# Dilated attention on even tokens, then odd ones, two heads at a time in the array's halves

## The chip, the core and the metric

The kernel runs on one core of a Trainium2 chip. The metric is the device time of one execution in microseconds (us); the profile's times are those of one profiled execution. Engines: TensorE (PE; PEld is its weight load), VectorE (DVE), ScalarE (ACT), GpSimd (POOL), SyncE (SP, which issues most DMAs).

## What is computed

A network on 256 tokens of 1024 channels: gated feed-forwards, a forgetting attention, a dilated attention and two mixing layers, all in float32. The change concerns the dilated attention (16 heads of 64 channels, three groups):

```python
DIL_CONFIGS = ((128, 1), (512, 4), (2048, 16))      # window, dilation

def dilated_group(q, k, v, window, dilation):
    # query t attends t, t-d, t-2d, ..., t-window
    ...
    logits = jnp.einsum("bqhd,bqkhd->bhqk", qb, kb) * scale
    logits = jnp.where(valid, logits, -jnp.inf)
    lse = jax.nn.logsumexp(logits, axis=-1)
    ob = jnp.einsum("bhqk,bqkhd->bqhd", jnp.exp(logits - lse), vb)
    return ob, lse

for g, (window, dilation) in enumerate(DIL_CONFIGS):
    q = apply_rope(rms_norm(proj[:, :, g, 0], q_gain[g]), cos, sin)
    k = apply_rope(rms_norm(proj[:, :, g, 1], k_gain[g]), cos, sin)
    o, lse = dilated_group(q, k, proj[:, :, g, 2], window, dilation)
alpha = softmax(lses over the groups)
o = sum(alpha * outs)          # then o @ w_out
```

The merge over the groups equals one softmax over the keys of all three groups, and so it is computed. With dilations 4 and 16 a query at an even token only sees keys at even tokens, one at an odd token only odd ones.

## The kernel before

Channels lie on partitions, tokens along the free axis. Every weight is split into two float32r parts (`whi` by ScalarE, `wlo` by VectorE, one pair for each unit of 128 x 1024), and each projection is three TensorE products: `hh,whi`, `hl,whi`, `hh,wlo` (for values `whi,hh` and so on; `oh` and `ol` hold the attention's outputs for the last projection). These are called plain products here. Everything else runs beside them: generators (`dil_qk`, `dil_norm`, `dil_head`) yield until the class `Clock` estimates that an instruction's operands are there, and so the order on every engine is fixed when the program is built. All instructions pass through one helper, so the profile gives one line for them all (L415), and the groups are told apart by tiles: `qk` are logits, `cst,ar` transposes, `ar` on 128*64 the outputs, `cst,rs` the spreading of the inverse sums.

In `dil` the queries and keys of two heads (a pair) come from three projection tiles; `head_in` and `head_norm` norm them, `dil_norm` turns them (rotary embedding, VectorE). `dil_head` then handles one head: six float32 products give the logits of queries 0 to 127 with keys 0 to 127 and of queries 128 to 255 with all 256 keys, in each of three groups, in three neighbouring banks of PSUM; VectorE adds the mask `dm` and takes the row minimum (two masked sums of 384 and 768 columns); ScalarE takes the exponential with its sum; TensorE transposes nine tiles of 128 x 128, ScalarE copies them back, TensorE multiplies them with the values (`pv`) and spreads the inverse sums (`inverse`). Head e of a pair has its channels on partitions 64 e to 64 e + 63, so its logits use the upper or lower half of the array's rows, and its outputs one half of the array's columns. `P` is held twice, so that the two heads of a pair overlap. `o_store` copies output and inverse (`ot`), multiplies them and splits the product into `oh` and `ol`. `attn_out` runs the last projection in four steps of two pairs, waiting until these are stored; `residual` adds it to `x` and prepares the next norm.

Of the kernel before, what the change touches and what calls it, by code (L numbers as in the profile page):

```python
# [26 lines left out]
I32 = mybir.dt.int32  # L27
# [39 lines left out]
def _weights(seg):  # L67
    """Chunks of one part of the network, each of one or two units: (key, number of units)."""
# [58 lines left out]

# which layer's modulation is worked out beside which of the first blocks
# [102 lines left out]
# columns of the tile that holds one value per channel  # L231
# [9 lines left out]
# columns of the tile of constants  # L241
# [8 lines left out]
# columns of the small matrices of a mixing layer  # L250
# [40 lines left out]
def _host_cst():  # L291
# [10 lines left out]
    d0, d1 = [], []  # L302
    for window, dil in ((128, 1), (512, 4), (2048, 16)):
        d0.append(np.where(ok0 & (q - cols[:, :128] <= window) & ((q - cols[:, :128]) % dil == 0), 0, NEG))
        t = q + 128
        d1.append(np.where(ok1 & (t - cols <= window) & ((t - cols) % dil == 0), 0, NEG))
    dm = np.ascontiguousarray(np.concatenate(d0 + d1, axis=1), np.float32)
# [74 lines left out]
GAP = 400               # the least wait of VectorE that is filled  # L382
QUIET = 9               # from which chunk of the last rows no weights are prepared
QUIET_POST = 1
RESIDUAL_AT = 2         # chunk of rows at which the residual's operands are prepared
ORDER = (0, 2, 1, 3, 4, 6, 5, 7)
# after which chunks of the products ahead of a norm's scale come sums of squares, all of them, the scale, and weights
LEAD = ({2: (None,)}, 2, 3, (2, 3))
LEAD_POST = ({6: (None,)}, 6, 7, (6, 7))
NRAW = 4                # chunks of weights that are loaded ahead  # L390
NU = 7                  # units of weights that are prepared ahead
UNIT = 1024


class Engine:
    """An engine's instructions, with an estimate of when they are done."""
# [24 lines left out]
class Clock:  # L421
    """Passes instructions on to the core's engines, and estimates (in ns) when their operands are there and
    when they are done, from shapes alone: the order of what runs beside the projections follows it."""

    GRAIN = 512
    LATE = {"pe": 60, "dve": 250, "act": 360, "pool": 200, "dma": 100}     # until other engines see a result
# [30 lines left out]
    def grains(self, ap):  # L457
        """The parts of a tile that an operand touches."""
# [7 lines left out]
    def ready(self, name, ins=(), outs=()):  # L466
        """When engine name can read ins and write outs."""
# [25 lines left out]
    def fill_gap(self, name, ins, outs):  # L493
        """Emits what can fill VectorE's time until an instruction's operands are there."""
# [19 lines left out]
    def tile(self, pool):  # L514
        """pool.tile, which records when the slot of a new tile gets free."""
# [24 lines left out]
class Stream:  # L540
    """The weights, in the order in which they are used: each is loaded ahead, and split into the part
    that float32r holds and the rest, which float32r holds as well."""

    def __init__(self, k, dram):
# [38 lines left out]
    def step(self, limit):  # L583
        """Prepares the next unit, if there is room for it."""
# [58 lines left out]
    def need(self, l, blk):  # L643
        """Emits what computes the modulation's tile blk of layer l."""
# [8 lines left out]
class K:  # L653
    def __init__(self, tc, ctx, a, out):
# [6 lines left out]
        self.free = set(range(8))      # banks of PSUM  # L661
# [25 lines left out]
    # -- small helpers -----------------------------------------------------  # L687
# [26 lines left out]
    def mm(self):  # L714
        """A bank of PSUM, for the projections."""
# [3 lines left out]
    def mm4(self):  # L719
        """Four banks that leave four neighbouring ones."""  # L720
# [1548 lines left out]
```

## Time and profile before

| | |
|---|---|
| median of 3 runs | 1943.55 us (1941.72 to 1943.92) |
| span of the profiled execution (no other time is given for it) | 1946.9 us |
| TensorE busy | 1891.6 us, 97% |
| VectorE busy | 1488.4 us, 76% |
| ScalarE busy | 1013.4 us, 52% |

The dilated block lies between about 767 and 1124 us. Busy shares are means over stages with different limits, so the stretch itself has to be read. A record of TensorE has a modelled end and overlaps the next one; what a product costs in a row of them is read from start to start. The granted clock is a share of full speed: 1.00 is 2.4 GHz, 0.50 is 1.2 GHz.

### The profile page before, as it was taken

To read this page: it belongs to the slowest core of one execution; us is meant where nothing else is said; L and a number is where in the kernel's file an instruction comes from. 1 tells how busy PE (TensorE), PEld (TensorE's weight loads), DVE (VectorE), ACT (ScalarE), POOL (GpSimd) and SP (SyncE) were. 2 spreads that over 40 slices of the span, in tenths; PEclk is the share of its full clock that TensorE was granted. 3 is DMA by queue.
4 is the path that set the end of the run, shared out by engine and by line. 5 is a ranking of instruction groups with operands and counts; after the bars stand their busy time and mean duration, and the time that the engine had idled before them with its cause. 6 is when DMAs were issued, how large, how long until landed. Compare 5 with 4: busy or idle time off the path is not lost.

```text
span 1946.9 us, 36564 instructions
## 1 busy us (share of the span) xinstructions
PE 1891.6 (97%) x15150; PEld 1814.4 (93%) x15150; DVE 1488.4 (76%) x2706; ACT 1013.4 (52%) x1721; POOL 35.5 (2%) x40
## 2 busy tenths in 40 slices
PE   6999999999999999999999999999999998999997
PEld 6999987899999999999989899999889998989997
DVE  6987795598779876767777585569779778969876
ACT  3534644554355445554455464444666555466553
POOL 0100000000000000000000000000000000000000
PEclk9999989999999999999999999999989998999998
DMA  9798373289858973433324175535236543325550
GB/s 373 298 350 322 131 282 109 93 306 362 326 178 298 341 298 130 174 115 125 130 88 143 74 261 205 212 130 188 94 128 217 186 157 127 137 84 191 199 195 23
DMA packets 54167, 378.67 MB, mean 194 GB/s; under 512 B 6096, under 2 KB 7600, under 8 KB 9072
## 3 DMA queue, kind: packets, MB, share of 16 engines
q1 hardware_dynamic: 52992, 373.20, 52.2%
q0 software_dynamic: 864, 3.00, 0.5%
q8 instruction: 118, 1.93, 0.4%
q14 instruction: 49, 0.40, 0.1%
q10 hardware_dynamic: 144, 0.13, 0.0%
HBM read 375.21 MB, written 1.05 MB: 193 GB/s over the span
## 4 chain that ended last, share of the span: by engine, by line
PE 72%; issue 20%; DVE 4%; ACT 2%; POOL 1%; DMA 0%; POOLq 0%; SPq 0%; DVEq 0%; ACTq 0%
PE banks L415 72%; DVE ar L415 1%; DVE wlo L415 1%; POOL rz L415 1%; DVE x L415 1%; ACT whi L415 1%; ACT hh L415 0%; DVE sq L415 0%; DMA x<-x 0%; DVE hl L415 0%; DVE ht L415 0%; ACT sq L415 0%; ACT L415 0%; DVE wraw L415 0%; ACT ar L415 0%
## 5 line engine op out<-in xcount | busy, mean ns | idle before, releaser
L415 PE MATMUL banks<-hh,whi 128*128 128x256 f32 (+1 forms) x2792 | 799.2, 286 | 7.6 <-ACT hh L415 4.7
L415 DVE TENSOR_TENSOR wlo<-wraw,whi 128x1024 fp32r<-128x1024 f32 x557 | 670.2, 1220 | 171.2 <-ACT whi L415 170.6
L415 PE MATMUL banks<-hh,wlo 128*128 128x256 f32 (+1 forms) x2792 | 789.4, 283 | 2.0 <-DVE wlo L415 2.0
L415 PE MATMUL banks<-hl,whi 128*128 128x256 f32 (+1 forms) x2792 | 790.1, 283 | 0.2
L415 ACT CAST whi<-wraw 128x1024 fp32r<-128x1024 f32 x557 | 570.3, 1048 | 177.5 <-DMA wraw<-w 92.2
L415 PEld LDWEIGHTS banks<-hh,whi 128*128 128x128 f32 x2792 | 531.2, 190 | 13.5 <-ACT hh L415 5.5
L415 PEld LDWEIGHTS banks<-hh,wlo 128*128 128x128 f32 x2792 | 531.2, 190 | 2.8 <-DVE wlo L415 2.8
L415 PEld LDWEIGHTS banks<-hl,whi 128*128 128x128 f32 x2792 | 531.4, 190 | 1.1 <-DVE hl L415 1.1
L415 PE MATMUL banks<-oh,whi 128*128 128x256 f32 x1312 | 372.7, 284 | 7.3 <-DVE x L415 3.8
L415 PE MATMUL banks<-ol,whi 128*128 128x256 f32 x1312 | 366.8, 280 | 0.0
L415 PE MATMUL banks<-oh,wlo 128*128 128x256 f32 x1312 | 366.4, 279 | 0.0
L415 PEld LDWEIGHTS banks<-oh,whi 128*128 128x128 f32 x1312 | 247.2, 188 | 14.0 <-DVE x L415 6.3
L415 PEld LDWEIGHTS banks<-ol,whi 128*128 128x128 f32 x1312 | 247.5, 189 | 0.2 <-DVE ol L415 0.2
L415 PEld LDWEIGHTS banks<-oh,wlo 128*128 128x128 f32 x1312 | 247.2, 188 | 0.0
L415 DVE CUSTOM_DVE_ANT_0 wraw<-wraw,cb 128x1024 f32<-128x1024 f32 x128 | 152.0, 1217 | 0.5 <-DMA wraw<-w 0.5
L415 ACT ACTIVATE sg<-banks 128x256 f32<-128x256 f32 x82 | 31.5, 385 | 175.4 <-PE banks L415 175.3
L415 PE MATMUL banks<-whi,hh 128*128 128x256 f32 x352 | 106.0, 301 | 1.6 <-ACT hh L415 1.4
L415 PE MATMUL banks<-whi,hl 128*128 128x256 f32 x352 | 101.3, 288 | 0.1
L415 PE MATMUL banks<-wlo,hh 128*128 128x256 f32 x352 | 100.9, 287 | 0.0
L415 ACT COPY ar<-banks 128x384 f32<-128x384 f32 (+5 forms) x110 | 47.4, 477 | 99.3 <-PE banks L415 96.0
L415 PE MATMUL banks<-ar 128*64 128x256 f32 (+4 forms) x456 | 90.9, 335 | 0.0
L415 DVE SCALAR_TENSOR_TENSOR cy<-cs,vec,cy 128x255 f32<-128x255 f32 (+1 forms) x176 | 83.7, 481 | 7.8 <-ACT cy L415 4.7
(204 smaller groups left out, 1790.5 us busy)
## 6 DMA issues: line engine op xcount, KB each, us to landing
wraw<-w SPq DMA_DIRECT2D x342, 1024.0 KB, 4.9
ar<-w SPq DMA_DIRECT2D x8, 1024.0 KB, 10.4
wraw<-w SPq DMA_DIRECT2D x5, 512.0 KB, 3.4
ar<-lw POOLq DMA_DIRECT2D x2, 752.0 KB, 5.0
x<-x SPq DMA_DIRECT2D x1, 1024.0 KB, 7.2
out<-x SPq DMA_DIRECT2D x8, 128.0 KB, 1.9
cst<-cst SPq DMA_DIRECT2D x1, 595.5 KB, 6.1
ar<-dm POOLq DMA_DIRECT2D x1, 576.0 KB, 10.4
```

Source lines behind the costliest of these rows:

```text
L415: return f(out, *args, **kw)
```

## The change

The tokens are put in another order for the dilated block: even ones first, then odd ones. The norm ahead of it reads `x` in that order, the rotary tables are made in it, and the residual behind it writes `x` back in the old order. Now queries 0 to 127 are the even tokens and 128 to 255 the odd ones; group 0 (dilation 1) takes all 256 keys for each, groups 1 and 2 one tile of 128 keys. A generator handles a pair of heads at once, with each product of the first head next to the same one of the second. A masked sum now has 512 columns, and there are four for a pair; there are 16 transposes for a pair instead of 18. One pair is in flight at a time.

```diff
+def parted(ap):
+    return ap.rearrange("p (i b) -> p b i", b=2)
+def halves(ap):
+    return ap.rearrange("p (b i) -> p b i", b=2)
...
-    def make_h(self, rb, g, shift=None, ks=range(8)):
+    def make_h(self, rb, g, shift=None, ks=range(8), part=False):
+        order, same = (parted, halves) if part else (lambda t: t,) * 2
-            nc.vector.scalar_tensor_tensor(t, self.x[:, k], g[:, k:k + 1], rb[:, :S], op0=OP.mult, op1=OP.mult)
+            nc.vector.scalar_tensor_tensor(same(t), order(self.x[:, k]), g[:, k:k + 1], order(rb[:, :S]), op0=OP.mult,
+                                           op1=OP.mult)
...
-            nc.scalar.activation(self.hh[:, k], self.x[:, k], AF.Copy, scale=g[:, k:k + 1])
+            nc.scalar.activation(same(self.hh[:, k]), order(self.x[:, k]), AF.Copy, scale=g[:, k:k + 1])
...
+            x = order(self.x[:, m])
+            nc.vector.scalar_tensor_tensor(x, same(acc[bank][:, m % 2 * 256:m % 2 * 256 + 256]), gate[:, m:m + 1], x,
+                                           op0=OP.mult, op1=OP.add)
...
+    def inverse2(self, out, rs):
+        for qt in range(2):
+            for e in range(2):
+                self.nc.tensor.matmul(out[64 * e:64 * e + 64, qt * 128:qt * 128 + 128],
+                                      rs[:, 2 * e + qt:2 * e + qt + 1].to_broadcast([128, 64]), self.c("ident"),
+                                      start=True, stop=True, skip_group_check=True)
...
+    def dil_heads(self, c, qks, dv, vready, pvs):
+        while self.busy:
+            yield
...
+        for qt in range(2):
+            q = slice(qt * 128, qt * 128 + 128)
+            L = yield from self.bank(2)
+            for g, c0, keys in ((0, 0, slice(S, 2 * S)), (1, 256, slice(S + qt * 128, S + qt * 128 + 128)),
+                                (2, 384, slice(S + qt * 128, S + qt * 128 + 128))):
+                for e, r in enumerate(half):
+                    nc.tensor.matmul(L[:, e, c0:c0 + keys.stop - keys.start], qks[g][r, q], qks[g][r, keys], start=True,
+                                     stop=True)
+            for e in range(2):
+                p = P[:, e, qt * 512:qt * 512 + 512]
+                yield from self.on("dve", L[:, e], out=[p])
+                nc.vector.tensor_tensor_reduce(p, L[:, e], self.dm[:, qt * 512:qt * 512 + 512], -1.0, CAP, OP.add, OP.min,
+                                               nm[:, 2 * e + qt:2 * e + qt + 1])
...
+        for i, (g, kt) in enumerate(((0, 0), (0, 1), (1, 0), (1, 1), (2, 0), (2, 1))):
+            for e in range(2):
+                o = pv[64 * e:64 * e + 64, :S] if g == 0 else pv[64 * e:64 * e + 64, kt * 128:kt * 128 + 128]
...
+                nc.tensor.matmul(o, dv[:, g, kt, vh:vh + 64], p, start=i == 0, stop=g == 2, skip_group_check=True)
+        self.busy.remove(0)
+        self.inverse2(pv[:, S:], rs)
```

Where this stands in TensorE's order, at the logits of the second pair (`qk` with its number is the tile of a group, three of them; `hh`, `hl`, `whi`, `wlo` are a projection). Before:

```order
L415 MATMUL banks_70<-hh_74,wlo_9278 128x256
L415 MATMUL banks_70<-qk_8858 128x128
L415 MATMUL banks_70<-qk_8858 128x256
L415 MATMUL banks_70<-qk_8859 128x128
L415 MATMUL banks_70<-qk_8859 128x256
L415 MATMUL banks_70<-qk_8860 128x128
L415 MATMUL banks_70<-qk_8860 128x256
```

The second head's six follow in the same way. After:

```order
L425 MATMUL banks_70<-hh_74,wlo_9306 128x256
L425 MATMUL banks_70<-qk_8858 128x256 x2
L425 MATMUL banks_70<-qk_8859 128x128 x2
L425 MATMUL banks_70<-qk_8860 128x128 x2
L425 MATMUL banks_70<-qk_8858 128x256 x2
L425 MATMUL banks_70<-qk_8859 128x128 x2
L425 MATMUL banks_70<-qk_8860 128x128 x2
L425 MATMUL banks_70<-hh_74,whi_9305 128x256
```

Every x2 is the first head's product and the second's; the first three rows are the even queries, the next three the odd ones.

On ScalarE, at the end of the block, around the outputs of the last pair (`ar` from banks are the transposes copied back, `ot` output and inverse, `oh` what the last projection reads, `whi` a weight cast). Before:

```order
L415 CAST whi<-wraw 128x1024
L415 COPY ar<-banks 128x384
L415 COPY ot<-banks 128x512
L415 CAST whi<-wraw 128x1024
L415 CAST oh<-ot 128x256
```

After:

```order
L425 COPY ar<-banks 128x512 x4
L425 CAST whi<-wraw 128x1024
L425 CAST hh<-modc 128x8x2
L425 COPY ot<-banks 128x512
L425 CAST whi<-wraw 128x1024 x3
L425 CAST oh<-ot 128x256
```

Three weight casts instead of one now stand between `ot` and `oh`.

## Rows read from the trace of the kernel before

**Rows 1.** Busy time by stretch, attention part and after the idle time; first row: columns
```profile
core 0: us, PE busy (x) PEld busy (x) DVE busy (x) ACT busy (x) POOL busy (x), PEclk, DMA share, GB/s
780.00:1104.60 324.60, 324.60 (x2481) 297.75 (x2479) 231.18 (x439) 162.18 (x291) 0.00 (x0) 1.00 0.35 124
...
1107.70:1111.10 3.40, 3.31 (x14) 3.14 (x15) 1.64 (x4) 0.76 (x3) 0.00 (x0) 0.50 0.84 308
```
**Rows 2.** Waits of TensorE, 767 to 1104 us: total us, times, longest
```profile
PE banks L415 <- POOL rz L415: 0.4, 1, 0.4
```
**Rows 3.** Timeline of TensorE (start, us, instruction): logits of two heads, of one
```profile
898.70 3.65 PE L415 MATMUL banks<-qk 64*128 64x128 f32 x24
...
1082.44 0.28 PE L415 MATMUL banks<-oh,wlo 128*128 128x256 f32 x1
...
1082.80 0.28 PE L415 MATMUL banks<-oh,wlo 128*128 128x256 f32 x1
1083.01 2.23 PE L415 MATMUL banks<-qk 64*128 64x128 f32 x12
```
**Rows 4.** Timeline of TensorE: outputs, inverses, transposes of one head
```profile
908.85 2.17 PE L415 MATMUL banks<-ar 128*64 128x256 f32 x12
910.85 0.60 PE L415 MATMUL banks<-cst,rs 128*64 128x128 f32 x4
911.38 1.20 PE L415 MATMUL banks<-cst,ar 128*128 128x128 f32 x9
912.41 0.27 PE L415 MATMUL banks<-cst,ypad 128*96 128x128 f32 x1
```
**Rows 5.** Timeline of TensorE in a mixing layer, outputs on either 64 partitions
```profile
1332.90 1.14 PE L415 MATMUL banks<-ar,sv 128*64 128x128 f32 x16
1333.97 0.48 PE L415 MATMUL banks<-ar 128*128 128x256 f32 x1
```
**Rows 6.** Chain that ended last (start, us, what), and TensorE's timeline at its end
```profile
1104.12 0.59 ACT ot L415
1104.71 0.95 ACT whi L415
...
1105.68 1.22 DVE wlo L415
1106.91 0.35 DVE ot L415
...
1107.33 0.41 ACT oh L415
...
1107.79 0.58 PE L415 MATMUL banks<-oh,whi 128*128 128x256 f32 x1 [3.15 <-ACT oh L415]
```
**Rows 7.** Groups, 800 to 1104 us: count | busy us, mean ns | idle before
```profile
L415 DVE TENSOR_TENSOR wlo<-wraw,whi 128x1024 fp32r<-128x1024 f32 x65 | 78.4, 1220 | 28.8 <-ACT whi L415 28.7
L415 DVE TENSOR_TENSOR qk<-qk,ar 128x512 f32<-128x512 f32 x24 | 16.6, 692 | 0.8
L415 DVE CUSTOM_DVE_ANT_0 ar<-banks,ar 128x768 f32<-128x768 f32 x16 | 15.2, 953 | 0.0
L415 DVE CUSTOM_DVE_ANT_0 ar<-banks,ar 128x384 f32<-128x384 f32 x16 | 8.9, 556 | 15.8 <-PE banks L415 15.8
...
L415 ACT CAST whi<-wraw 128x1024 fp32r<-128x1024 f32 x64 | 65.8, 1058 | 0.2
L415 ACT ACTIVATE ar<-ar,nm 128x768 f32<-128x768 f32 x16 | 14.9, 934 | 1.1 <-DVE nm L415 1.0
```
**Rows 8.** Busy time by stretch in the forgetting attention, columns as in rows 1
```profile
240.00:280.00 40.00, 38.30 (x278) 35.04 (x277) 39.21 (x84) 24.35 (x42) 2.95 (x6) 0.94 0.79 288
274.80:285.00 10.20, 10.20 (x45) 9.29 (x44) 9.93 (x31) 3.92 (x10) 0.00 (x0) 0.50 0.64 237
```
**Rows 9.** Groups, 754 to 782 us, at the norm ahead of the dilated attention
```profile
L415 ACT ACTIVATE hh<-x,modc 128x256 fp32r<-128x256 f32 x6 | 3.0, 508 | 3.2 <-DVE x L415 3.2
...
L415 DVE SCALAR_TENSOR_TENSOR x<-banks,modc,x 128x256 f32<-128x256 f32 x5 | 2.4, 474 | 0.0
```

More of the change, by code (lines that the diff above doesn't have):

```diff
@@ L301, in _host_cst @@
     c["causal"] = np.concatenate([np.where(ok0, 0, NEG), np.where(ok1, 0, NEG)], axis=1)
[L302 to L307, printed above, removed]
+    dm = []
+    for qt in range(2):
+        for (window, dil), keys in zip(((128, 1), (512, 4), (2048, 16)), (range(2), (qt,), (qt,))):
+            for kt in keys:
+                lag = 2 * q + qt - (2 * np.arange(128)[None, :] + kt)
+                dm.append(np.where((lag >= 0) & (lag <= window) & (lag % dil == 0), 0, NEG))
+    dm = np.ascontiguousarray(np.concatenate(dm, axis=1), np.float32)
     row = np.arange(128) % 32
@@ L943, in mod, with ahead @@
         return self.modc[:, i + 1], self.modc[:, i]
-    def ahead(self, lead, g, shift):
+    def ahead(self, lead, g, shift, part=False):
         nc = self.nc
@@ L951, in ahead @@
         add, end, fold, merge = self.squares(st)
+        order, same = (parted, halves) if part else (lambda t: t,) * 2
         if shift is not None:
@@ L957, in high @@
         def high(k):
[L958 removed]
+            nc.scalar.activation(same(self.hh[:, k]), order(self.x[:, k]), AF.Copy, scale=g[:, k:k + 1])
         def low(k):
[L961 to L964 removed]
+            nc.vector.scalar_tensor_tensor(same(self.hl[:, k]), order(self.x[:, k]), g[:, k:k + 1],
+                                           same(self.hh[:, k].bitcast(F32)), op0=OP.mult, op1=OP.subtract)
+        return add, merge, fold, high, low, (st, end, g, shift, lead, part)
     def begin(self, norm, checks, lazy=False):
         nc = self.nc
[L970 removed]
+        st, end, g, shift, lead, part = norm
         n = S if shift is None else SX
@@ L993, in begin @@
                 self.st.step(NU)
-        nc.scalar.copy(self.rb, rb[:, :S])
+        if part:
+            nc.scalar.copy(halves(self.rb), parted(rb[:, :S]))
+        else:
+            nc.scalar.copy(self.rb, rb[:, :S])
         if not lazy:
-            self.make_h(rb, g, shift, ORDER)
+            self.make_h(rb, g, shift, ORDER, part)
         self.rel(rb)
@@ L1042, in rows, with residual @@
         self.quiet = False
-    def residual(self, gate, *following):
+    def residual(self, gate, following, part=False):
         nc = self.nc
+        order, same = (parted, halves) if part else (lambda t: t,) * 2
         self.qm = QUIET
-        add, merge, fold, high, low, norm = self.ahead(LEAD, *following)
+        add, merge, fold, high, low, norm = self.ahead(LEAD, *following())
         late = []
@@ L1206, in ffn @@
                            {1: self.rope_tables, 2: lambda: self.mix_ahead(0)}[l + j]() if l else None)
[L1207 removed]
+        norm, after = self.residual(self.gate(l, s, 0.5), following)
         end(after)
@@ L1216, in attn_out @@
             if c == RESIDUAL_AT:
-                norm, after = self.residual(gt, *following())
+                norm, after = self.residual(gt, following, part=l == 1)
             for half in range(2):
@@ L1525, in dil_qk @@
         ready[i] = "in"
-    def dil_head(self, h, qks, dv, vready, pvs):
+    def dil_heads(self, c, qks, dv, vready, pvs):
         nc = self.nc
-        e = h % 2
-        r = slice(64 * e, 64 * e + 64)
-        P, pT = self.PP[e], self.PT
-        while e in self.busy:
+        half = [slice(0, 64), slice(64, 128)]
+        P, X = self.P2, self.X2
+        while self.busy:
             yield
-        self.busy.add(e)
-        nm, sm, rs = self.small(2, "nm"), self.small(2, "sums"), self.small(2, "rs")
+        self.busy.add(0)
+        nm, sm, rs = self.small(4, "nm"), self.small(4, "sums"), self.small(4, "rs")
@@ L1537, in dil_head @@
         yield from self.on("pe", *qks)
-        L = yield from self.bank(3)
-        for g in range(3):
-            qk = qks[g]
-            nc.tensor.matmul(L[:, g, 0:128], qk[r, 0:128], qk[r, S:S + 128], start=True, stop=True)
-            nc.tensor.matmul(L[:, g, 128:384], qk[r, 128:256], qk[r, S:2 * S], start=True, stop=True)
-        yield from self.on("dve", L, out=[P])
-        for qt, c0, o, n in ((0, 0, 0, 128), (1, 384, 128, 256)):
-            v3 = lambda t: t[:, c0:c0 + 3 * n].rearrange("p (g n) -> p g n", g=3)
-            nc.vector.tensor_tensor_reduce(v3(P), L[:, :, o:o + n], v3(self.dm), -1.0, CAP, OP.add, OP.min,
-                                           nm[:, qt:qt + 1])
@@ L1554, in dil_head @@
+        self.logits += 2
+        for qt in range(2):
+            for e in range(2):
+                i, p = slice(2 * e + qt, 2 * e + qt + 1), P[:, e, qt * 512:qt * 512 + 512]
+                yield from self.on("act", p)
+                nc.scalar.activation(p, p, AF.Exp, scale=-1.0, bias=nm[:, i], accum_out=sm[:, i])
         yield from self.on("dve", sm)
         nc.vector.reciprocal(rs, sm)
-        while self.turn != h or not all(vready):
-            yield
-        yield from self.on("pe", P)
@@ L1559, in dil_head @@
-        for g in range(3):
-            T = yield from self.bank()
-            for b, c0 in enumerate((g * 128, 384 + g * 256, 512 + g * 256)):
-                nc.tensor.transpose(T[:, b * 128:b * 128 + 128], P[:, c0:c0 + 128], self.c("ident"))
-            yield from self.on("act", T[:, 0:384], out=[pT[:, g * 384:g * 384 + 384]])
-            nc.scalar.copy(pT[:, g * 384:g * 384 + 384], T[:, 0:384])
-            self.rel(T)
-        self.busy.remove(e)
-        yield from self.on("pe", pT, rs)
@@ L1568, in dil_head @@
-        pv = yield from self.pv_bank(h, pvs)
-        vh = slice(h % 4 * 64, h % 4 * 64 + 64)
-        self.pv(pv[r, :S], [(dv[:, g, kt, vh], pT[:, g * 384:g * 384 + 384], kt) for g in range(3) for kt in range(2)])
-        self.turn = h + 1
-        self.inverse(pv[r, S:], rs)
-        if e:
-            yield from self.o_store(pvs, h, h // 2, True)
-            self.stored.add(h // 2)
+        pT = [(X[:, 0:512], X[:, 512:1024]), (X[:, 1024:1536], P[:, 0, 0:512])]
+        for e in range(2):
+            for j in range(2):
+                yield from self.on("pe", P[:, e])
+                T = yield from self.bank()
+                for i in range(4):
+                    o = i % 2 * 512 + j * 256 + i // 2 * 128
+                    nc.tensor.transpose(T[:, i * 128:i * 128 + 128], P[:, e, o:o + 128], self.c("ident"))
+                yield from self.on("act", T, out=[pT[e][j]])
+                nc.scalar.copy(pT[e][j], T)
+                self.rel(T)
@@ new lines, in dil_heads @@
+        while not all(vready):
+            yield
+        yield from self.on("pe", *pT[0], *pT[1], rs)
+        pv = yield from self.bank()
+        for i, (g, kt) in enumerate(((0, 0), (0, 1), (1, 0), (1, 1), (2, 0), (2, 1))):
+            for e in range(2):
+                o = pv[64 * e:64 * e + 64, :S] if g == 0 else pv[64 * e:64 * e + 64, kt * 128:kt * 128 + 128]
+                p = pT[e][0][:, kt * 256:kt * 256 + 256] if g == 0 else pT[e][1][:, (2 * g - 2 + kt) * 128:(2 * g - 1 + kt) * 128]
+                vh = (2 * c + e) % 4 * 64
+                nc.tensor.matmul(o, dv[:, g, kt, vh:vh + 64], p, start=i == 0, stop=g == 2, skip_group_check=True)
@@ L1577, in dil @@
+        self.busy.remove(0)
+        self.inverse2(pv[:, S:], rs)
+        pvs[c] = pv
+        yield from self.o_store(pvs, 2 * c, c, True)
+        self.stored.add(c)
     def dil(self, norm, following):
```

29 lines of the change are left out of this document (8 added, 21 removed).

## The prediction

> **What bounds the kernel now.** I read the stretch table first: from 780 to 1104.6 us, the attention part of the dilated block, TensorE's records cover 324.60 of 324.60 us at a granted clock of 1.00, while VectorE is busy 231.18 us and ScalarE 162.18 us [rows 1]. Then I read who waits: between 767 and 1104 us TensorE waited for another engine once, for 0.4 us [rows 2]. So TensorE alone bounds this stretch, and a microsecond taken from it there is a microsecond of the kernel as long as nothing else comes late. Only after it does TensorE stand idle: 3.15 us before the last rows of the output projection, released by ScalarE's `oh` [rows 6], after which the clock is granted at 0.50 for 3.4 us [rows 1], the lower of its two levels, 1.2 instead of 2.4 GHz.
>
> A plain projection product (256 columns, float32r) starts 0.12 us after the one before it: three in 1082.44 to 1082.80 [rows 3]. A float32 product leaves two records. One head's logits, six products of 3 x 128 + 3 x 256 = 1152 columns, are busy for 2.23 us (x12); two heads back to back for 3.65 us (x24) and not 4.46, so they overlap at the seam only [rows 3]. One head's outputs, again 1152 columns, take from 908.85 to 910.85 = 2.00 us, the spreading of the inverse sums to 911.38 = 0.53 us, and nine transposes to 912.41 = 1.03 us, 0.114 us each [rows 4].
>
> **The change part by part.** The order of before has two heads' logits together for five of the eight pairs, and apart for the other three: 5 x 3.65 + 6 x 2.23 = 31.6 us. Outputs and inverses: 16 x 2.53 = 40.5 us.
>
> Do halves run at once? Two rows bear on it. In the mixing layer sixteen records of 128 columns, whose outputs lie on either 64 partitions of one bank, run from 1332.90 to 1333.97 = 1.07 us [rows 5], where sixteen of them one after another, at the 0.114 us of a transpose of as many columns, would need 1.8: eight steps of 0.11 and 0.2 us at the edges. That is the column half. The seam of the logits above, 0.81 us saved where one head's rows 64 to 127 follow the other's 0 to 63, is the row half. The change alternates the halves product by product, so I take full overlap.
>
> Logits then: per head 2 x (256 + 128 + 128) = 1024 columns, both heads at once: 2.23 x 1024/1152 = 1.98 us a pair, 15.9 in all, 15.8 saved. Outputs: 512 + 4 x 128 = 1024 columns, 2.00 x 1024/1152 = 1.78, with the inverses 0.53, at once for two heads: 2.31 x 8 = 18.5 us, 22.0 saved. Transposes: 128 instead of 144, 16 x 0.114 = 1.8 us saved. The step into a burst of half-array products costs 0.09 us more than a plain one (1082.80 to 1083.01 is 0.21, not 0.12) [rows 3]; the order holds 9 + 8 such bursts instead of 11 + 16, 0.9 us saved. TensorE's work shrinks by 40.5 us. The projections, and what belongs to the norms of the heads, are the same in number.
>
> The Trainium skill's page "TensorE: Matmul & The Clock Gate", section "Measured speedup vs the span model", gives 2.38 times for three column tiles and 3.07 for four row tiles, so about 0.78 per tile. By that (an estimate) two halves give 1.56 times, and the 34.4 us of logits, outputs and inverses would become 44.1, 9.7 us less saved; the sixteen records above come nearer to 2.
>
> The tail. Before, TensorE had three plain products left after the last inverse and then waited 3.15 us, since from 1104.12 the chain is the copy `ot` 0.59, a weight split on ScalarE 0.95, one on VectorE 1.22, VectorE's product 0.35, `oh` 0.41, until 1107.79 [rows 6]. In the changed order 30 plain products of earlier rows stand between the last inverse and those three: 33 x 0.12 = 4.0 us of cover. But ScalarE now has three weight casts between `ot` and `oh`. At 1.06 us each [rows 7] `oh` comes 0.59 + 3.2 + 0.41 = 4.2 us after the inverse, and `ol` behind two of VectorE's splits, some 0.4 later. I take 0.7 us of idle time (ends 0, and 3.15 as before): 2.5 us saved. Idle of that size should leave the clock alone, as the wait of 0.4 us did [rows 2], behind which the stretch stands at 1.00; so the 3.4 us at 0.50, which held 14 products [rows 1] where 28 fit at 0.12, give back another 1.7. Together 4.2 us.
>
> VectorE. Its masked sums take 0.953 + 0.556 us a head now [rows 7]; four of 512 columns, between these at about 0.69, take 2.8 a pair instead of 3.0. So VectorE keeps nearly all its 231 us in a stretch of 284: 81% on average, but not evenly. From the fifth pair's last logits to the eighth pair's first, TensorE's order holds 426 plain products (51 us) and some 26 us of the rest; VectorE's holds 18 weight splits of 1.22 = 22, 45 operations of the rotation at about 0.69 = 31, ten masked sums = 7, and some 13 us of smaller things: 73 us against 77. That is where waits can come: in the other attention, with VectorE busy for 39.21 of 40 us, TensorE was busy for 38.30 [rows 8], 4% lost. 4% of 77 is 3 us, which I take; the ends are 0 (the whole stretch of before) and 4% of all 284 = 11.
>
> One pair is in flight at a time. From the end of its logits to its last exponential the chain is at most 0.7 + 4 x 0.93 - 0.9 = 3.5 us by [rows 7] (one masked sum, four exponentials one after another, less the second half's logits); the order puts at least 42 plain products there, 5.0 us. Queued behind are only its 16 transposes on TensorE, four copies on ScalarE and then its outputs. Covered.
>
> The permutation. Reading or writing every other token changes eight operations each of `x`, `hh` and `hl` at two norms, and of `ht` in the first products: now 474 to 508 ns [rows 9], all on unit steps, so their price isn't shown. Ends: nothing, as the counts and sizes stay; twice as long. Doubled `x` (0.47 to 0.95, with `hl` 0.47 beside it) makes 1.42 us per tile where six plain products take 0.72, about 4 us at the end of the dilated block; the two other places have products to hide behind, 2 us at most. I take 0.5, near nothing, since two neighbouring values still lie 8 bytes apart. The Trainium skill's page "SBUF — State Buffer", section "Door 1: The DMA port swizzle", counts lines of 16 bytes, each of which a stride of two float32 still hits twice, so nothing by that page for SBUF; PSUM's lines are 8 bytes, which speaks against `ht`, whose second operand is read there. No run here shows it.
>
> Sum: 40.5 + 4.2 - 3.0 - 0.5 = 41.2 us saved. The profiled execution shows a span of 1946.9 us and no time of its own beside it; the median of the runs is 1943.55, 3.4 us less. The sum is made against the span, 1905.7 us, and the same difference gives **1902** us for the median.
>
> **The rivals.** (a) The halves overlap in part. If the 0.2 us that I put down to the edges in [rows 5] belong to the steps, sixteen records take 1.07 of 1.83 us, 0.58 and not 0.50 of the serial time; the 34.4 us become 40, 5.8 more: 1908. For it: no row has two different 256-column streams in column halves. Against: edges of 0.09 us show at other bursts [rows 3]. The Trainium skill's section on measured speedups, named above, would make it 1912 by its own figures (an estimate).
> (b) One of the two kinds doesn't overlap at all, and the change doesn't do what it says. Logits one after another cost 16 x 1.98 = 31.7, nothing saved: 1918. Outputs one after another cost 16 x 2.31 = 37, 3.5 saved: 1921.
> (c) VectorE becomes the bound of the whole stretch: 4% of 284 us, 11 instead of 3: 1910. For it: 73 against 77 us at the end. Against: in the first four of the seven steps from pair to pair VectorE's work, counted the same way, stays some 10% or more under TensorE's.
> (d) Slower. The shared buffers let only one pair run, so if the masked sums stand behind late weight splits, TensorE waits ahead of the transposes, and the clock falls behind each wait. Price: 3.15 us of idle [rows 6] and, as in the other attention, 10.2 us at 0.50 [rows 8], which costs 5.1: eight times 8.3 is 66, less the 3 counted: 1965. It decides from a chain 3 us later than its 5.0 us of cover, that is 8 us at every pair; by [rows 7] two weight splits ahead of it add 2.4 to 3.5.
> (e) The clock falls without idle time: in the other attention it did, TensorE busy for 10.20 of 10.20 us at 0.50 [rows 8], just behind logits on 64 rows. Eight times 5.1 is 41: 1943, no change. Against: 324.60 us of the same kind here stayed at 1.00 [rows 1], and the halves are now used together.
>
> **How the numbers follow.** Forecast 0.71; (a) 0.07; (b) 0.07; (c) 0.10; (d) 0.03; (e) 0.02. The forecast's own ends: with no waits and no stride price 1898, and 2 to 3 us lower or higher as the low-clock stretches of later blocks shift in length (1.7 us is what one of 3.4 us costs); with 11 us of waits and 6 of strides 1916. The range is 1895 to 1916: it holds the forecast, (a) and (c), 0.88 in all, and leaves out (b), (d), (e). About 0.2% is what a measurement of this kernel can tell from no change: faster 0.95, within it 0.02, slower 0.03.
>
> **What would show it.** In the changed kernel's trace: pairs of `qk` records starting within 0.02 us of each other, and a pair's logits in about 2 us; 24 output and 8 inverse records in about 2.3 us; the stretch from the first `qk` product to the end of the output projection shorter by 40 us or more; the 3.15 us wait for `oh` under 1.5 and the clock at 1.00 behind it; TensorE's waits for VectorE and ScalarE in the stretch at 3 us in total. It is wrong if the halves' records follow one another, if those waits pass 11 us, or if `x` with the new order takes over 0.6 us.

## The result, and the profile after

| | median of the runs | profiled execution, span |
|---|---|---|
| before | 1943.74 us (1941.72 to 1946.37, 4 runs) | 1946.9 us |
| after | 1900.46 us (1899.46 to 1904.99, 4 runs) | 1903.2 us |

The changed kernel takes 0.9776 of the time of the one before (95% interval 0.976 to 0.9792). Five more runs on another chip gave 1902.15 us, 0.978 of the kernel before beside them (0.9761 to 0.9798). The forecast was 1902, with a range of 1895 to 1916.

I call "the block" what lies between TensorE's two products `cst,rz`, at the norm ahead of the dilated attention and at the norm behind its output projection. It ran from 767.52 to 1122.70 us before, 355.18 us, and runs from 765.82 to 1080.41 after, 314.59 us: **40.6 of the 43.7 us of span** are saved there.

The stretch table after (columns as in [rows 1]) covers the attention part, the idle time at its end, and what follows that:

```profile
778.00:1062.60 284.60, 283.20 (x2456) 268.23 (x2456) 223.83 (x430) 156.78 (x277) 0.00 (x0) 1.00 0.39 138
1062.60:1067.40 4.80, 3.19 (x26) 2.91 (x25) 4.00 (x7) 1.69 (x4) 0.00 (x0) 1.00 0.77 249
1067.40:1070.80 3.40, 3.40 (x18) 3.40 (x18) 2.38 (x6) 2.29 (x6) 0.00 (x0) 0.51 0.63 265
```

TensorE is still covered nearly throughout, and VectorE has come closer: 223.83 of 284.60 us, 79%, where [rows 1] had 71%. The two heads of a pair are seen in TensorE's timeline (start, us, instruction), against [rows 3] and [rows 4]:

```profile
1020.43 2.03 PE L425 MATMUL banks<-qk 64*128 64x256 f32 x24
...
1028.75 1.91 PE L425 MATMUL banks<-cst,ar 128*128 128x128 f32 x16
...
1038.61 1.96 PE L425 MATMUL banks<-ar 128*64 128x256 f32 x24
1040.40 0.61 PE L425 MATMUL banks<-cst,rs 128*64 128x128 f32 x8
1040.94 0.39 PE L425 MATMUL banks<-oh,whi 128*128 128x256 f32 x1
```

Two heads' logits take 2.0 us where one head's took 2.23 [rows 3], and from the first of 24 output and 8 inverse records to the next product it is 1038.61 to 1040.94, 2.33 us, where 12 and 4 took 2.53 [rows 4]. The groups of these lines over the whole attention part say the same; before and after, count | busy us, mean ns of one record:

```profile
L415 PE MATMUL banks<-ar 128*64 128x256 f32 x192 | 34.6, 330 | 0.0
L415 PE MATMUL banks<-qk 64*128 64x128 f32 (+1 forms) x192 | 31.6, 332 | 0.0
...
L415 PE MATMUL banks<-cst,rs 128*64 128x128 f32 x64 | 9.6, 273 | 0.0
```
```profile
L425 PE MATMUL banks<-qk 64*128 64x128 f32 (+1 forms) x192 | 16.5, 316 | 0.0
L425 PE MATMUL banks<-ar 128*64 128x128 f32 (+1 forms) x192 | 15.7, 312 | 0.0
...
L425 PE MATMUL banks<-cst,rs 128*64 128x128 f32 x64 | 4.9, 273 | 0.0
```

A record is nearly as long as before (312 and 316 ns for 330 and 332, since a head has fewer columns, and 273 for the inverses in both), and as many of them cover half the time: they lie on top of each other.

Who waits in the block, after (us in total, times, longest), against [rows 2] and the 3.15 us of [rows 6]:

```profile
PE banks L425 <- DVE ol L425: 1.6, 1, 1.6
PE banks L425 <- DVE x L425: 0.8, 2, 0.4
PE banks L425 <- POOL rz L425: 0.8, 2, 0.4
PE banks L425 <- ACT hsq L425: 0.7, 1, 0.7
PE banks L425 <- DVE ypad L425: 0.5, 1, 0.5
PE banks L425 <- DVE qk L425: 0.2, 1, 0.2
```

To see where 40.6 us come from I added up, over the block, the time from the start of each record on TensorE to the start of the next, by kind of record, in both traces:

| | before | after | saved | forecast |
|---|---|---|---|---|
| logits `qk` | 30.85 | 15.84 | 15.0 | 15.8 |
| outputs `ar` and inverses `rs` | 40.50 | 18.59 | 21.9 | 22.0 |
| transposes `cst,ar` | 15.39 | 13.65 | 1.7 | 1.8 |
| output projection with its waits | 30.58 | 27.64 | 2.9 | 4.2 (tail) + 0.3 (3 of the 10 steps into bursts) |
| the rest, new waits among it | 237.86 | 238.87 | -1.0 | 0.6 (the other 7) - 3.0 (waits) - 0.5 (strides) |

### The profile page after: what moved, and what is told of

Its sections match the earlier page's. It is cut to its first block, busy times and chain, and to the rows that moved or that the text cites. A ratio compares the mean times of both kernels' runs of the same rounds, so it can differ in the third digit from the quotient of the medians.

```text
span 1903.2 us, 36479 instructions
## 1 busy us (share of the span) xinstructions
PE 1849.3 (97%) x15134; PEld 1784.4 (94%) x15134; DVE 1481.7 (78%) x2698; ACT 1007.5 (53%) x1705; POOL 35.5 (2%) x40
## 4 chain that ended last, share of the span: by engine, by line
PE 64%; issue 27%; DVE 5%; ACT 2%; POOL 1%; DMA 0%; POOLq 0%; SPq 0%; DVEq 0%; ACTq 0%
PE banks L425 64%; DVE wlo L425 1%; POOL rz L425 1%; DVE ar L425 1%; DVE x L425 1%; ACT whi L425 1%; DVE hl L425 0%; DVE sq L425 0%; ACT hh L425 0%; DMA x<-x 0%; DVE ht L425 0%; ACT sq L425 0%; ACT L425 0%; DVE rs L425 0%; DVE wraw L425 0%
## 5 line engine op out<-in xcount | busy, mean ns | idle before, releaser
L425 DVE TENSOR_TENSOR sg<-banks,sg 128x256 f32<-128x256 f32 x82 | 34.4, 422 | 69.4 <-ACT sg L425 69.3
L425 ACT COPY ar<-banks 128x512 f32<-128x512 f32 (+5 forms) x94 | 43.9, 513 | 68.8 <-PE banks L425 65.5
```

Source lines behind the costliest of these rows:

```text
L425: return f(out, *args, **kw)
```

## The experiments

**One head's logits, then the other's.** The pairs of neighbours are taken apart within a tile of queries.

```
-for g, c0, keys in (...):
-    for e, r in enumerate(half):
+for e, r in enumerate(half):
+    for g, c0, keys in (...):
         nc.tensor.matmul(L[:, e, ...], qks[g][r, q], qks[g][r, keys], ...)
```

> The changed kernel with one edit: within a tile of queries the three logits products of one head are issued together and then the three of the other, where the changed kernel issues the two heads in turn. Same products, same banks. Theory (the gain is that records of the two halves stand beside each other in the queue and run at once): the logits of the dilated stretch, 15.8 us of TensorE in the changed kernel, go back to about 28 (1024 columns of each of 16 heads at the rate of before), so about 12 us more, some 1913 us. Rival (the engine takes records of the other half out of its queue well ahead, as the two heads in a row of the kernel before suggest, 3.65 us where two single ones are 4.46, so 0.8 us ahead, which is a whole head's part of a tile here): 0 to 3 us more, 1900 to 1904.

Measured: 1906.8 us (1906.05 to 1908.66), ratio to before 0.9805 (0.9789 to 0.9822). The logits take 22.09 us of the block by the sums above, 6.25 more than in the changed kernel, and the block 4.4 more. That is between the two expectations, and neither stands as written. The block grew less than the logits mainly because the clock stays at 1.00 at its end here: behind the same wait of 1.61 us for `ol` it takes 13.32 us to its end, and 14.50 in the changed kernel; a wait of 0.51 us for `ypad` is gone as well. A pair's logits in TensorE's timeline:

```profile
916.52 2.77 PE L425 MATMUL banks<-qk 64*128 64x256 f32 x24
```

2.77 us is neither 2.03 nor the 3.5 that the expectation has for two heads in a row (28 / 8). Record by record, the second head's first record begins at 917.065, 0.006 us after the first head's third of six (917.059): the other half overtakes, but not from the start.

**One head's outputs, then the other's**, and so with the inverses:

```
-for i, (g, kt) in enumerate(((0, 0), (0, 1), (1, 0), (1, 1), (2, 0), (2, 1))):
-    for e in range(2):
+for e in range(2):
+    for i, (g, kt) in enumerate(((0, 0), (0, 1), (1, 0), (1, 1), (2, 0), (2, 1))):
```

> The changed kernel with one edit: the six output products of one head are issued together and then the six of the other, and so with the inverses. Theory (only neighbours overlap): outputs and inverses, 18.6 us in the changed kernel, go back to about 36, so about 18 us more, some 1918 us. Rival (the queue looks 0.8 us ahead at the seam of the two heads): 8 times 0.8 us less than that, about 12 us more, 1912. Rival (the pace was VectorE's and not TensorE's): under 5 us more.

Measured: 1914.12 us (1911.06 to 1914.52), ratio 0.9841 (0.9825 to 0.9856), 12 to 14 us above the two medians of the changed kernel; the block is 325.32, 10.7 more. The outputs take 23.05 us instead of 14.30 and the inverses 6.35 instead of 4.29, together 29.40; sixteen heads wholly apart take 28.60 and 8.48 (next but one experiment), so 0.96 us a pair still overlaps, at two seams. The rival with the look-ahead is right, and its length can be counted where the inverses of the first head (`cst,rs`) follow the outputs of the second (`ar`):

```profile
911.24 0.93 PE L425 MATMUL banks<-ar 128*64 128x256 f32 x6
911.90 0.32 PE L425 MATMUL banks<-cst,rs 128*64 128x128 f32 x1
912.01 0.27 PE L425 MATMUL banks<-ar 128*64 128x128 f32 x1
...
912.12 0.27 PE L425 MATMUL banks<-ar 128*64 128x128 f32 x1
...
912.22 0.27 PE L425 MATMUL banks<-ar 128*64 128x128 f32 x1
```

The first inverse starts at 911.90 beside an output record that is still counted in the group above it, and three more outputs start behind it. So it ran when four records, two float32 products, of the other half were left, the one that starts beside it counted, and no earlier. At the seam of the two heads' outputs it is four too: the second head's first record starts at 910.545, 0.006 us after the ninth of the first head's twelve. In the logits of the kernel above it is four as well (the third to the sixth of six), and so it already is in the kernel before, in the two heads of [rows 3]: 900.117, 0.006 us after the ninth of twelve. There two of the four have 256 columns, and the overlap lasts some 0.65 us; between the outputs here all four have 128, and it lasts 0.43 (910.545 to 910.976). So it is a number of records and not a time.

**The outputs in turns of two products** tests that count:

```
+for g in range(3):
+    for e, kt in ((0, 0), (0, 1), (1, 0), (1, 1)):
```

> The changed kernel with the output products in turns of two: two products of one head (four records), two of the other, and so on. With all six of a head together the other head's first record started when four records of the first stood before it, and 0.7 us a pair overlapped. Theory A (a record of the other half starts once no more than four records stand before it in its neighbour's half): turns of two overlap as fully as turns of one, the outputs' 14.3 us stay, 0 to 1 us more, about 1901 us. Theory B (the overlap at a seam is an end effect of fixed length, and the turns of one are needed): six seams a pair where there were twelve neighbours, about half of the gain in the outputs lost, 6 to 7 us more, 1907 us.

Measured: 1901.33 us (1900.67 to 1903.83), ratio 0.9776 (0.9761 to 0.979), with the outputs at 14.30 us as in the changed kernel and the inverses at 4.70, 0.41 more.

```profile
1035.88 2.01 PE L425 MATMUL banks<-ar 128*64 128x256 f32 x24
1037.66 0.66 PE L425 MATMUL banks<-cst,rs 128*64 128x128 f32 x8
```

Theory A holds: strict alternation isn't needed, turns of four records overlap as fully but for 0.05 us a pair behind the last turn.

**The token order alone**, one head at a time as before: the changed masks, 1024 columns and the strided norms stay, the functions for a pair of heads go back to those for one.

```
-self.dil_heads(2 * c + e, qks, dv, vready, pvs)
+for i in range(2):
+    self.dil_head(4 * c + 2 * e + i, qks, dv, vready, pvs)
```

> The token order alone: even tokens, then odd ones, with one tile of keys for dilations 4 and 16 (1024 columns a head), but one head at a time as in the kernel before. Theory (most of the gain is two halves at once): what is left is 1152 to 1024 columns in the logits (30.9 to 27.4 us) and in the outputs (32.0 to 28.5) and 9 to 8 transposes (1.7 us), 8.6 us off the kernel before, 1935 us (1932 to 1939). Rival (the shorter work of the new order, with VectorE and ScalarE too, is the larger part): 20 us or more off, under 1924.

Measured: 1932.96 us (1931.04 to 1935.47), ratio 0.9942 (0.9925 to 0.9958), 11.4 us under the 1944.38 of before beside it; the block is 345.67, 9.5 less, and the other 1.9 lie outside it. Logits 26.95 us (expected 27.4), outputs 28.60 (28.5), transposes 13.56.

**The halves alone**, tokens in their old order:

```
+for q, groups, n, c0 in ((slice(0, 128), (0, 1, 2), 128, 0),
+                         (slice(128, 256), (0, 1), 256, 384), (slice(128, 256), (2,), 256, 896)):
     for k, g in enumerate(groups):
         for e, r in enumerate(half):
             nc.tensor.matmul(L[:, e, k * n:k * n + n], qks[g][r, q], qks[g][r, S:S + n], ...)
```

> The halves alone: two heads at a time with their products in turn as in the changed kernel, but tokens in their old order with 1152 columns a head, nine transposes, and the second tile of queries in two bites (dilations 1 and 4, then 16), with one small minimum more a pair. Theory: against the changed kernel the logits cost 15.8 times 1/8 = 2.0 us more, the outputs 1.8, the transposes 1.7, eight more bursts of logits about 0.2 us each, 1.6: 7 us more, 1907 us (1904 to 1912). Rival (the new order is the larger part): 15 us or more above the changed kernel, over 1915.

Measured: 1911.25 us (1909.11 to 1911.86), ratio 0.9827 (0.9813 to 0.9842): within the range given, above its middle. The block is 320.80, 6.2 more than after and 34.4 less than before. Logits 17.93 (2.1 more), outputs 16.01 (1.7 more), transposes 16.98 (3.3 more, 1.2 of it two waits, 0.77 and 0.40, for their copies `ar`). The halves are the larger part, and the two parts nearly add up: 9.5 and 34.4 are 43.9; the dropped columns saved 7.3 us in the logits and outputs of the first and would save half of that with the heads on top of each other, so 40.2, where the change has 40.6. The block's time at half clock isn't the same in all four: 3.4 us before and after, 6.8 in the order alone and none in the halves alone, so 9.5 is somewhat too little for the order and 34.4 somewhat too much for the halves.

**Work added on VectorE.** The rest asks how much room VectorE has left.

```
+for i in range(4):
+    nc.vector.tensor_tensor(self.t512("sh"), qks[i % 3], qks[i % 3], op=OP.add)
+    yield
```

> The changed kernel with work added that nothing reads: four additions of 512 columns on VectorE for each pair of heads, 32 in all, about 0.5 to 0.7 us each, 16 to 22 us of VectorE more in a stretch where it is busy 224 of 285 us. Theory (TensorE sets the pace of the stretch and VectorE has room): under 3 us more. Rival (VectorE has become the bound, which would cap the gain of the change): 8 us or more.

Measured: 1911.9 us (1910.3 to 1913.26), ratio 0.9832 (0.9818 to 0.9845), some 10 us more; the block is 325.27, 10.7 more. My theory of room to spare is wrong for the kernel as it is then built. The additions took 0.683 us each, 21.9 in all. Two stretches and TensorE's waits:

```profile
778.00:1057.00 279.00, 275.23 (x2374) 261.12 (x2373) 233.97 (x445) 149.22 (x259) 0.00 (x0) 1.00 0.38 140
1057.00:1074.00 17.00, 10.82 (x67) 8.49 (x67) 9.44 (x19) 6.09 (x14) 0.00 (x0) 0.60 0.35 124
```
```profile
1057.31 0.56 PE L425 MATMUL banks<-qk 64*128 64x128 f32 x4 [2.45 <-DVE qk L425]
1061.79 2.69 PE L425 MATMUL banks<-qk 64*128 64x256 f32 x12 [3.93 <-DVE nm L425]
1066.13 3.46 PE L425 MATMUL banks<-cst,ar 128*128 128x128 f32 x15 [1.25 <-ACT ar L425]
```

For 279 us TensorE stays covered to all but 3.8 us, and then the last pair's chain stands open: its rotation comes late (2.45), its masked sums hold the banks of the second half's logits (3.93), and the clock of that stretch is 0.60.

Then the same additions for the **first five pairs alone** and for the **last three alone**:

> Four additions of 512 columns on VectorE, whose results nothing reads, for the first five pairs of heads alone (20 of the 32 that cost 10 us together). Theory (VectorE has room while products stand ready, and only the last pairs' chain of norm, logits and masked sums is short of it): 0 to 2 us more than the changed kernel, 1900 to 1903. Rival (VectorE paces the whole stretch once it is that full): 20 of 32 of 10 us, 6 to 7 us more, 1907.

> The same additions for the last three pairs alone (12 of the 32, 8.2 us of VectorE). Theory (only the last pairs' chain is short of VectorE): 6 to 10 us more than the changed kernel, 1907 to 1911. Rival (VectorE paces the whole stretch): 12 of 32 of 10 us, 4 us more or less, 1905.

Measured: early 1907.4 us (1905.49 to 1910.73), block 318.30, 3.7 more for 13.7 us of VectorE; late 1907.26 us (1904.47 to 1910.78), block 320.29, 5.7 more for 8.2 us. The late ones cost what the theory said, at its lower edge; the early ones should have cost at most 2 us, and by the time of the runs they cost as much as the rival said, by the block about half of it. So the theory falls in its first half. But no wait of more than 0.4 us shows among the first five pairs, as the rival would have it: the early ones' price too is paid by the last pair. Its logits come in two halves here, 36 plain products lie between them (4.5 us), and its transposes wait for the exponentials:

```profile
1052.96 1.15 PE L425 MATMUL banks<-qk 64*128 64x256 f32 x12
...
1058.55 1.75 PE L425 MATMUL banks<-qk 64*128 64x256 f32 x12
1062.89 3.24 PE L425 MATMUL banks<-cst,ar 128*128 128x128 f32 x15 [2.33 <-ACT ar L425]
```

So VectorE doesn't pace the stretch; the price falls at its end, where no products are left to cover the last pair. But these three kernels differ from the changed one in more than VectorE's load: the estimate of `Clock` counts the additions too, and so TensorE's order is another. Of the 192 plain products of the output projection the changed kernel has 42 ahead of the last pair's logits, 72 between these and its outputs, and 78 behind. With the early additions 108 stand ahead, 36 between the two halves of the logits, none from there to the outputs, and 48 behind; with the late ones it is 126, 18, none and 48, with all of them 144, none, none and 48. How much of the price is VectorE's time and how much is this order, the runs don't separate. That the early work is still owed at the end isn't shown: in the 15 us in which the last pair's rotation begins, VectorE is busy for 8.45 us with the early additions (second row) and for 12.49 in the changed kernel (first row).

```profile
1030.00:1045.00 15.00, 14.79 (x127) 13.18 (x125) 12.49 (x22) 6.40 (x9) 0.00 (x0) 1.00 0.36 121
1030.00:1045.00 15.00, 15.00 (x134) 13.73 (x133) 8.45 (x15) 8.42 (x15) 0.00 (x0) 1.00 0.40 141
```

**The tail.** TensorE's 1.6 us wait for `ol` was the place where the forecast was off. After, ScalarE and VectorE at the end of the last pair:

```profile
1060.13 0.59 ACT L425 COPY ot<-banks 128x512 f32<-128x512 f32 x1 [2.09 <-PE banks L425]
1060.61 2.95 ACT L425 CAST whi<-wraw 128x1024 fp32r<-128x1024 f32 x3
1061.69 1.23 DVE L425 TENSOR_TENSOR wlo<-wraw,whi 128x1024 fp32r<-128x1024 f32 x1 [3.44 <-ACT whi L425]
1062.84 0.42 DVE L425 TENSOR_TENSOR ot<-ot 128x256 f32<-128x256 f32 x1
1063.17 2.35 DVE L425 TENSOR_TENSOR wlo<-wraw,whi 128x1024 fp32r<-128x1024 f32 x2
1063.45 0.41 ACT L425 CAST oh<-ot 128x256 fp32r<-128x256 f32 x1
1065.44 0.42 DVE L425 TENSOR_TENSOR ol<-ot,oh 128x256 fp32r<-128x256 f32 x1
...
1065.91 0.38 PE L425 MATMUL banks<-ol,whi 128*128 128x256 f32 x1 [1.61 <-DVE ol L425]
```

The output rows `oh` are there at 1063.86, but `ol` stands behind two weight splits of 2.35 us. Three kernels hold the split of the next stage's weights back: between `ot` and `ol` (first), until the last sum of the residual is out (second), or over both except for the two that come right behind `ol` (third).

```
 self.inverse2(pv[:, S:], rs)
+self.hold = c == 7
 yield from self.o_store(pvs, 2 * c, c, True)
+self.hold = False
...
 def tick(self):
+    if self.hold:
+        return
```

The second clears `hold` in `after(m)` at m = 7 instead; the third clears it here too, and sets it again in `after(m)` for m from 0 to 6.

> The changed kernel, but while the last pair's outputs are scaled and split no weights of the next stage are split (nothing stands between `ot` and `ol` on VectorE or between `ot` and `oh` on ScalarE). Theory (TensorE's wait of 1.61 us for `ol` is the two weight splits that VectorE does between): the wait falls to about 0.7 us, and if a wait of that length leaves the granted clock at 1.00 the 3.4 us at half clock behind it go too: 1 us less for the wait, up to 1.7 more for the clock, 1897.5 to 1899.5. Rival (the weights put off are then late themselves): the wait moves to the split weights behind it, no gain or a loss of 1 to 2 us.

> The changed kernel, but no weights of the next stage are split from the last pair's outputs until the last sum of the residual is out (before, they were let in again once `ol` was written, and one of them stood before a sum that freed a bank, a new wait of 2.4 us). Theory: that wait falls below 0.6 us, 1.8 us less than with the earlier end of the hold, the granted clock stays at 1.00 behind it, 1898 to 1900. Rival (the next stage's first products then wait for their weights): a wait of 1 us or more for `whi` or `wlo` behind it, no gain.

> As the first hold (no weights of the next stage split between `ot` and `ol` of the last pair), and let in again after `ol` as there, but held once more from the first sum of the residual to the last; against that run exactly one `wlo` goes from between two sums to behind the last. Theory: its wait of 2.43 us for `x` falls to about 0.6, the weights split before the first sum last until the next ones are there, no new wait; the dilated block takes 1.8 us less than with the first hold, 311.9 us where the changed kernel has 314.5, and the time is 1898 to 1900. Rival (every split weight that is put off is missed at once, as with the hold over the whole tail, 2.4 and 1.6 us for `whi` and `wlo`): a wait of over 1 us for `whi` or `wlo`, the block at 313.7 or above.

Measured: first 1903.26 us (1901.12 to 1904.0), beside 1902.15 for the changed kernel on the same chip, block 313.67 against 314.42; second 1907.23 us (1904.54 to 1908.78), block 319.26; third 1907.63 us (1905.0 to 1909.24), block 315.61. Each time the wait for `ol` is gone and another stands in its place, one row of each kernel's timeline (of the second and third also the row after):

```profile
1071.15 0.39 PE L425 MATMUL banks<-oh,whi 128*128 128x256 f32 x1 [2.43 <-DVE x L425]
```
```profile
1069.24 0.39 PE L425 MATMUL banks<-hh,whi 128*128 128x258 f32 x1 [2.37 <-ACT whi L425]
1071.35 0.58 PE L425 MATMUL banks<-hh,wlo 128*128 128x258 f32 x1 [1.61 <-DVE wlo L425]
```
```profile
1073.86 0.39 PE L425 MATMUL banks<-hh,whi 128*128 128x258 f32 x1 [1.64 <-ACT whi L425]
1075.97 0.39 PE L425 MATMUL banks<-hh,wlo 128*128 128x258 f32 x1 [1.60 <-DVE wlo L425]
```

None of these kernels is faster than the changed one. In the second and third the rivals hold: the split weights that were put off are missed at once. In the first the rival is right on the gain and not on the place: TensorE waits for a sum of the residual, `x`, which stands behind a weight split on VectorE. So in the three places tried, the work between `ot` and `ol` could be moved but not avoided.

## Why the prediction was right, and where it was off

**TensorE alone bounds the stretch**: right. What was taken from its records, 38.7 us in logits, outputs, inverses and transposes, came off the block.

**Full overlap** is the step on which the forecast hung, and it held. From start to start a pair's logits take 15.84 / 8 = 1.98 us, the 1.98 of the working, and outputs with inverses 18.59 / 8 = 2.32, against 2.31. Rivals (a) and (b) are out. The section on measured speedups that the prediction named from the Trainium skill's page "TensorE: Matmul & The Clock Gate" would make two tiles 1.56 times as fast (an estimate, from its 2.38 times for three and 3.07 for four); the trace doesn't agree, 28.60 to 14.30 us is 2.00 times. The reading of the seam in [rows 3] as overlap of the row halves was right too, and the runs say more than the prediction did: the overlap there is four records long, so the change didn't need to alternate product by product.

**The logits' term was 0.8 us too large.** It started from 31.6 us of busy time, which counts the end of the last record of a burst, already under the next product; from start to start they took 30.85.

**The tail was mis-sized**, 4.2 us for what turned out 1.85: from the last inverse to the end of the block it took 18.68 us before and takes 20.40 after, with 30 more plain products at 0.119. (The other 1.1 of the table's 2.9 are fewer interruptions: the projection's products take a step of 0.20 us or more instead of 0.12 seven times ahead of the tail, and nineteen before.) The step that failed is the 0.7 us of idle time. The cover of 4.0 us was right (the inverses give way to plain products at 1060.01, and these end at 1064.3), and so was the late `oh`; but `ol` was put "some 0.4 later", and it came 2.0 us later than `oh`, since the two splits that the prediction names stand between `ot` and `ol` and not beside ScalarE's casts. The wait fell from 3.15 to 1.61 us. And the clock was not left alone: 0.51 for 3.4 us behind it, where [rows 1] had 0.50 for 3.4. So two of the prediction's signs, a wait under 1.5 us and the clock at 1.00 behind it, did not come. The 1.7 us put at the clock was too much as well: where it stays at 1.00 behind the same wait, the same 96 records take 13.32 us to the end of the block instead of 14.50, 1.2 less.

**VectorE's waits were too large**, 3 us for 1.4 (0.7 for `hsq`, which ScalarE writes, 0.5 and 0.2). The argument behind them, 73 us of work against 77 at the end of the stretch, fits the added work, where 8.2 us more cost 5.7, though in another order of products. Rival (c) may name the next bound, but it isn't one yet. Rivals (d) and (e) show nowhere: the clock is 1.00 up to 1062.6 us.

**The strides cost next to nothing.** Every other token is read by `hh`, `hl` and `ht` at the norm ahead of the dilated attention, and read and written by `x` at its residual. Ahead of the block, before and after (745 to 765 us), then `x` behind it after the change:

```profile
L415 ACT ACTIVATE hh<-x,modc 128x256 fp32r<-128x256 f32 x8 | 4.1, 508 | 6.3 <-DVE x L415 6.3
L415 DVE SCALAR_TENSOR_TENSOR hl<-x,modc,hh 128x256 fp32r<-128x256 f32 x8 | 3.8, 475 | 0.3 <-ACT hh L415 0.3
```
```profile
L425 ACT ACTIVATE hh<-x,modc 128x256 fp32r<-128x256 f32 x8 | 4.2, 524 | 6.3 <-DVE x L425 6.3
L425 DVE SCALAR_TENSOR_TENSOR hl<-x,modc,hh 128x256 fp32r<-128x256 f32 x8 | 3.8, 477 | 0.4 <-ACT hh L425 0.4
...
L425 DVE SCALAR_TENSOR_TENSOR x<-banks,modc,x 128x256 f32<-128x256 f32 x8 | 3.8, 480 | 1.9 <-PE banks L425 1.9
```

VectorE's operations take the same to 2 ns: `hl` 477 for 475, `x` 480 for 480, and `ht`, which reads its other operand from PSUM, 476 for 474. ScalarE's `hh` takes 16 ns more, in every run with the new order (523 to 526 ns, and 508 with the halves alone): 0.13 us in all, and TensorE doesn't wait for it. By the lines of 16 bytes in the Trainium skill's page "SBUF — State Buffer", section "Door 1: The DMA port swizzle", the prediction took nothing as the price in SBUF: VectorE's rows agree, ScalarE's 16 ns don't quite; that PSUM's narrower lines would speak against `ht` does not show.

**Some of the total is chance.** The terms give 38.7 + 2.9 - 1.0 = 40.6 for the block, 0.6 under the forecast's 41.2. That is close because errors cancel: the logits and the projection with its tail were put 2.4 us too high, the saving in the rest, where waits and strides were taken off, 1.9 too low. The other 3.1 us of the span lie ahead of the block (1.7) and behind it (1.4), where the change does next to nothing: stretches at the lower clock there are shorter (10.2 us became 6.8 in the forgetting attention, and likewise in a stretch some 300 us behind the block). In the 14 profiled executions of all these kernels the block begins anywhere from 761.59 to 767.52 us. So the median of 1900.46 under the forecast's 1902 is no evidence that the terms were too small.

## What to carry to other kernels

Products that use half of the array's rows or columns are worth pairing with the other half wherever TensorE alone bounds a stretch, and it is enough that the two stand within four records of each other. Size such a saving from start to start of the records and not from their busy time, and then ask who must be in time at the end of the stretch, where no products are left as cover: there 8.2 us of added work on VectorE cost 5.7. Where an estimate orders the instructions, added work changes the order too, so such a test must be read beside the order that it built. A wait at the seam of two stages that is filled with the next stage's preparation moves when that work is put off; it goes only when there is less of it.

## What the runs showed of the hardware

- In all four places read, one of them in the kernel before, a record for one half of the array starts once four records for the other half are left before it, the one that starts beside it counted: six output products of one head ahead of six of the other overlap by 0.43 us, turns of two products as fully as turns of one (14.30 us both).
- Two halves of the array's columns give back the whole factor: outputs 28.60 to 14.30 us, inverses 8.49 to 4.29.
- The same wait of 1.61 or 1.62 us at the tail is followed by 3.4 us at half clock in the changed kernel (both profiles) and with the outputs apart, and by none with the logits apart and with turns of two, here

```profile
1061.00:1066.00 5.00, 3.38 (x27) 3.11 (x26) 4.18 (x8) 1.35 (x4) 0.00 (x0) 1.00 0.95 324
1066.00:1070.00 4.00, 3.38 (x27) 2.98 (x26) 3.96 (x10) 2.97 (x7) 0.00 (x0) 1.00 0.28 119
```

  The length of the wait alone doesn't decide it, since a wait of 2.43 us in the first of the three held kernels left the clock at 1.00. What does was not tried, and stays open. So a forecast should hold both: 1.2 us either way.
- Reading PSUM and SBUF and writing SBUF at every other float32 costs VectorE nothing that shows (476 to 480 ns against 474 to 480); reading SBUF so costs ScalarE 16 ns on 508.
